# Second block of a fused two-block kernel: queries and keys projected and normed by token tile, taps queued behind fixed instructions, residual scaled on VectorE

## Chip, cores and metric

One core of a Trainium2 chip runs the whole program. The metric is the device time of one execution in microseconds; lower is better. The kernel before takes 1275.32 us (median of 3 runs, 1274.69 to 1275.57).

## What is computed

Two transformer blocks follow each other on 512 tokens of width 1024, in 32-bit floats. The change lies in the second block, up to its output projection:

```
h = rms_norm(x, norm1_g)
q, k, v, glu_a, glu_b = split(h @ w_in)           # 5 x 512 columns
q = rms_norm(q by head of 64, q_norm_g);  k the same with k_norm_g
attn = stick_breaking_attention(q, k, v)          # 8 heads, strictly causal
c = glu_a * sigmoid(glu_b)
c = causal_depthwise_conv(c, 31 taps);  c = silu(layer_norm(c))
x = x + concatenate([attn, c]) @ w_out
```

Here x is the first block's output, which ends in an rms norm of its own (final_norm_g); the kernel keeps it unnormed in `h` (tiles A) and multiplies by the token's factor later.

## The kernel before

Matrices are kept as a high and a low part (`copy_split`, `scale_split`), and a product of two of them is three matmuls (`mm3`, lines 123 to 125). Weights come by DMA into `raw` (two buffers), ScalarE casts them into `whi` (L195), VectorE subtracts to get `wlo` (L196); both have two buffers, so a cast waits until TensorE has read the last of an older weight tile. The token axis is the free axis of most tiles; queries and keys are first made with tokens on the partitions and then transposed.

In the second block `glu(i)` makes four 128-channel chunks of the gated product: 48 matmuls into a pair of PSUM banks, evacuation with the norm's factor (L693), sigmoid, product (L698) into `cc`. The convolution's 31 taps per chunk are one ScalarE instruction (L128) and 30 VectorE instructions (L832), each of which adds one tap to `cv[:, i, :]`; 120 in all, in an order that `conv` and `turns` give. `heads` makes queries (with `early[:2]` as weights, tiles F and G) and keys (tiles E and a fresh tile): `mov_stage` runs 96 matmuls for four token tiles of 128 into two pairs of banks, all four tiles for each half of the weights; then another `glu` (`between`) is issued; then for each pair of token tiles a square on ScalarE (L729), a sum by head on VectorE (L731), the power -0.5 on GpSimd in four instructions (L737 to L740, with the factors `rr` and `rr2` of the norm before), the product on VectorE (L741), eight transposes on TensorE (L745), and `scale_split` into the result (L139 on ScalarE, L140 on VectorE). Three PSUM pairs (`pair`) go round among all of these.

The attention stage behind it runs 12 steps (`seq`): `sticks` (scores, L774 and L779; abs, exponential and logarithm on ScalarE, L782 to L784; L785 and L132 on VectorE), `breaks` (L798, L801, exponential L803), `gather` (L813). Between them stand the remaining taps. `conv_norm` and `attended` (the output projection, L946 adds the residual) follow. The residual `h` is multiplied by `rb3`, the factor of the first block's last norm, in four GpSimd instructions (L871).

The program's order on each engine is made by the framework: it simulates the instructions as they are written and lets each engine take what is ready first; `tc.issue_after` puts an instruction behind another one in that order. Engines then run their queues in order, with waits on semaphores. The order is fixed when the program is built.

## Time and profile before

| | us |
|---|---|
| runs (median, lowest to highest of 3) | 1275.32 (1274.69 to 1275.57) |
| profiled execution | 1275.78 |
| its span, first to last instruction | 1274.1 |
| TensorE busy | 1257.1 |
| VectorE busy | 772.2 |
| ScalarE busy | 485.1 |
| GpSimd busy | 108.7 |

The second block's part up to the output projection lies between about 680 and 900 us of the span. In the timelines a row is: start, duration, engine, line, operation, output and inputs by tile, shapes, count of merged instructions, and in brackets the idle time ahead of it and who ended it. Matmuls overlap, so the distance between two starts, not a duration, is the rate. The granted clock (PEclk) is 1.00 at 2.4 GHz and 0.50 at 1.2 GHz.

### The profile page before, as it was taken

The page shows a single profiled execution, that of the slowest core. Times are in us where ns is not written, and L with a number is a line of the kernel's source. Part 1 is how long each engine was busy: PE and PEld are TensorE (multiplying, and loading weights), DVE is VectorE, ACT ScalarE, POOL GpSimd, SP SyncE. Part 2 cuts the span into 40 slices and gives each one's busy share as a digit, 9 for nine tenths or more (in the row PEclk, how much of TensorE's full clock was granted, in tenths as well). Part 3 has the DMA queues.
Part 4 walks back from the last instruction along what each step waited for, and adds up shares of the span by engine and source line. Part 5 has one row for each costly group of instructions (what it writes and reads, how often), then busy time and mean ns, then how long its engine had stood idle before and what let it go on. Part 6 is the DMA issues. An engine that isn't in the chain of part 4 may idle for free.

```text
span 1274.1 us, 13633 instructions
## 1 busy us (share of the span) xinstructions
PE 1257.1 (99%) x5712; PEld 1011.6 (79%) x5712; DVE 772.2 (61%) x813; ACT 485.1 (38%) x528; POOL 108.7 (9%) x125
## 2 busy tenths in 40 slices
PE   9999999999999999999999899999999999999998
PEld 6888888788888888888887678667888888888887
DVE  7845624744866664466366999976675555336522
ACT  6432524532544432243253225873443333213310
POOL 1100210012000000000054411000400000000000
PEclk9999999999999999999999989999999999999999
DMA  7233222312222222222343001101222222222212
GB/s 285 91 112 109 99 99 74 126 66 100 94 77 95 99 99 99 100 82 85 116 149 132 0 34 67 67 1 66 99 100 99 76 90 99 100 100 100 87 63 81
DMA packets 20445, 118.32 MB, mean 93 GB/s; under 512 B 2208, under 2 KB 4128, under 8 KB 7712
## 3 DMA queue, kind: packets, MB, share of 16 engines
q1 hardware_dynamic: 20096, 117.20, 26.1%
q8 instruction: 44, 0.72, 0.2%
q10 hardware_dynamic: 288, 0.26, 0.1%
q14 instruction: 17, 0.14, 0.0%
HBM read 115.35 MB, written 2.10 MB: 92 GB/s over the span
## 4 chain that ended last, share of the span: by engine, by line
PE 92%; DVE 4%; ACT 2%; issue 1%; POOL 1%; DMA 0%; SPq 0%; DVEq 0%; ACTq 0%
PE pp L124 28%; PE pp L125 28%; PE pp L123 28%; DVE H L832 2%; PE ps L123 1%; PE ps L124 1%; PE ps L125 1%; POOL col L739 0%; DVE H L698 0%; PE ps L317 0%; PE ps L813 0%; DVE t L785 0%; PE pp L774 0%; DMA A<-in_xT 0%; ACT t L783 0%
## 5 line engine op out<-in xcount | busy, mean ns | idle before, releaser
L195 ACT CAST whi<-raw 128x2048 fp32r<-128x2048 f32 (+3 forms) x109 | 197.8, 1815 | 452.4 <-PE pp L124 381.9
L196 DVE TENSOR_TENSOR wlo<-raw,whi 128x2048 fp32r<-128x2048 f32 (+3 forms) x109 | 236.8, 2173 | 73.2 <-ACT whi L195 72.6
L123 PE MATMUL pp<-B,whi 128*128 128x512 f32 x672 | 265.8, 397 | 1.0 <-ACT whi L195 1.0
L125 PE MATMUL pp<-B,wlo 128*128 128x512 f32 x672 | 266.3, 396 | 0.2
L124 PE MATMUL pp<-C,whi 128*128 128x512 f32 x672 | 266.0, 396 | 0.0
L124 PE MATMUL pp<-G,whi 128*128 128x512 f32 x448 | 177.8, 397 | 0.0
L125 PE MATMUL pp<-F,wlo 128*128 128x512 f32 x416 | 164.9, 396 | 0.0
L123 PE MATMUL pp<-F,whi 128*128 128x512 f32 x416 | 164.2, 396 | 0.0
L123 PEld LDWEIGHTS pp<-B,whi 128*128 128x128 f32 x672 | 126.3, 188 | 32.1 <-ACT whi L195 1.8
L125 PEld LDWEIGHTS pp<-B,wlo 128*128 128x128 f32 x672 | 126.2, 188 | 32.1 <-DVE wlo L196 1.5
L124 PEld LDWEIGHTS pp<-C,whi 128*128 128x128 f32 x672 | 126.3, 188 | 30.7 <-issue 0.5
L124 PEld LDWEIGHTS pp<-G,whi 128*128 128x128 f32 x448 | 84.2, 188 | 20.4 <-issue 0.2
L625 DVE TENSOR_TENSOR A<-pp,A 128x1024 f32<-128x1024 f32 x23 | 28.2, 1225 | 112.2 <-PE pp L125 112.2
L125 PEld LDWEIGHTS pp<-F,wlo 128*128 128x128 f32 x416 | 78.2, 188 | 19.0 <-issue 0.2
L646 DVE SCALAR_TENSOR_TENSOR H<-H,sm,H 128x512 f32<-128x512 f32 x132 | 92.8, 747 | 0.7
L123 PEld LDWEIGHTS pp<-F,whi 128*128 128x128 f32 x416 | 78.1, 188 | 19.0 <-issue 0.2
L832 DVE SCALAR_TENSOR_TENSOR H<-H,sm,H 128x512 f32<-128x512 f32 x120 | 88.3, 765 | 1.2
L651 DVE TENSOR_TENSOR H<-pp,rb 128x1024 f32<-128x1024 f32 x22 | 26.9, 1224 | 56.2 <-PE pp L125 49.8
L128 ACT ACTIVATE H<-H,sm 128x512 f32<-128x512 f32 x70 | 54.2, 808 | 9.8 <-DVE H L698 9.8
L997 DVE TENSOR_TENSOR H<-pp,rb 128x512 f32<-128x512 f32 x22 | 15.2, 692 | 67.7 <-PE pp L125 61.3
L124 PE MATMUL pp<-E,whi 128*128 128x512 f32 x112 | 44.3, 396 | 0.0
L123 PE MATMUL pp<-D,whi 128*128 128x512 f32 x112 | 44.2, 395 | 0.0
(293 smaller groups left out, 1808.8 us busy)
## 6 DMA issues: line engine op xcount, KB each, us to landing
raw<-in_wts SPq DMA_DIRECT2D x99, 1024.0 KB, 4.8
raw<-in_wts SPq DMA_DIRECT2D x8, 768.0 KB, 4.2
A<-in_xT SPq DMA_DIRECT2D x3, 512.0 KB, 6.8
out<-A SPq DMA_DIRECT2D x3, 512.0 KB, 2.8
D<-in_memT SPq DMA_DIRECT2D x1, 1024.0 KB, 11.6
raw<-in_wts SPq DMA_DIRECT2D x3, 256.0 KB, 7.1
A<-in_xT SPq DMA_DIRECT2D x2, 256.0 KB, 3.4
raw<-in_wts SPq DMA_DIRECT2D x2, 128.0 KB, 3.6
```

The lines of the kernel that those rows point to most:

```text
L123: pe.matmul(out, wh, xh, start=start, stop=False, **kw)
L124: pe.matmul(out, wh, xl, start=False, stop=False, **kw)
L125: pe.matmul(out, wl, xh, start=False, stop=stop, **kw)
L128: act.activation(out, in_, AF.Identity, scale=scale, bias=bias)
L195: act.copy(hi[:, cs], raw[:, cs])
L196: dve.tensor_tensor(lo[:, cs], raw[:, cs], hi[:, cs].bitcast(F32), ALU.subtract)
L625: dve.tensor_tensor(hu, pt, hu, ALU.add)
L646: dve.scalar_tensor_tensor(dst, hs[:, k : k + 512], w(k), dst, ALU.mult, ALU.add)
L651: dve.tensor_tensor(hs[:, :, 2:], pt, over2(rb), ALU.mult)
L832: tap = dve.scalar_tensor_tensor(cv[:, i, :], cc[:, i, k : k + 512], par("dw_w", 4 * k + i), cv[:, i, :], ALU.mult, ALU.add)
L997: dve.tensor_tensor(hs[:, 2:514], pt[:, 0, :], rb, ALU.mult)
```

## The change

`heads` now takes one token tile after the other (24 matmuls each, both halves of the weights) and issues square, sum, power and product for that tile at once, on 512 columns; GpSimd's four instructions become three with per-partition factors. `conv` takes its taps from one list, `TURNS`, which alternates between two chunks nearly throughout, and can be put behind a given instruction: 8 taps behind the first gated product, 6 behind the second, 5 behind each token tile's product of queries and keys and 5 behind the third and fourth gated product, the other 56 behind those. The residual's factor is applied on VectorE, written in `attended`. The diff, whole:

```diff
--- before.py
+++ after.py
@@ -695,7 +695,7 @@
         if i == 3:
             with tc.issue_after(sig.ins):
                 act.preload_act_table_set(tables)
-        dve.tensor_tensor(cc[:, i, 30:542], ab[:, 0, :], ab[:, 1, :], ALU.mult)
+        return dve.tensor_tensor(cc[:, i, 30:542], ab[:, 0, :], ab[:, 1, :], ALU.mult)
 
     rb2 = rb3 = None
 
@@ -716,33 +716,37 @@
 
     rr, rr2 = keep("rr"), keep("rr2")
 
-    def heads(name, gain, sc, between, early=()):
+    def heads(name, gain, sc, taps, between, early=()):
+
         gc = col(1)
         dve.tensor_scalar(gc, par(gain), sc, None, ALU.mult)
-        pts = mov_stage(ph, pl, NT, early)
+        ws = (list(early) + [weights() for _ in range(2 - len(early))])
         dst = [half(name + "0", 4, T), half(name + "1", 4, T)]
+        for t in range(NT):
+            if t % 2 == 0:
+                pt = pair()
+            ps = pt[:, t % 2, :]
+            st = slice(t * P, (t + 1) * P)
+            for k in range(KC):
+                wh, wl = (w[:, k % 4, :] for w in ws[k // 4])
+                mm3(ps, ph[:, k, st], pl[:, k, st], wh, wl, k == 0, k == KC - 1)
+            qn = norm2[:, t, :]
+            heads8 = qn.rearrange("p (b d) -> p b d", d=HD)
+            act.activation(qn, ps, AF.Square)
+            ms = tp.tile([P, 8], F32, tag="col16", name="col16", bufs=8)
+            dve.tensor_reduce(ms, heads8, AX.X, ALU.add)
+            pool.tensor_scalar(ms, ms, rr2[:, t : t + 1], EPS, ALU.mult, ALU.add)
+            pool.tensor_tensor(ms, ms, mhalf[:, :8], ALU.pow)
+            pool.tensor_scalar(ms, ms, rr[:, t : t + 1], None, ALU.mult)
+            conv(taps[t], dve.tensor_tensor(heads8, ps.rearrange("p (b d) -> p b d", d=HD),
+                                            ms.unsqueeze(2).to_broadcast([P, 8, HD]), ALU.mult))
         between()
         for i in range(2):
-            src = pts[i].rearrange("p a (b d) -> p (a b) d", d=HD)
-            qn = norm2[:, 2 * i : 2 * i + 2, :]
-            heads16 = qn.rearrange("p a (b d) -> p (a b) d", d=HD)
-            act.activation(qn, pts[i], AF.Square)
-            ms = col(16)
-            dve.tensor_reduce(ms, heads16, AX.X, ALU.add)
-            ms2 = ms.rearrange("p (a b) -> p a b", a=2)
-
-            def per_token(c):
-                return c[:, 2 * i : 2 * i + 2].unsqueeze(2).to_broadcast([P, 2, 8])
-
-            pool.tensor_tensor(ms2, ms2, per_token(rr2), ALU.mult)
-            pool.tensor_scalar(ms, ms, EPS, None, ALU.add)
-            pool.tensor_tensor(ms, ms, mhalf[:, :16], ALU.pow)
-            pool.tensor_tensor(ms2, ms2, per_token(rr), ALU.mult)
-            dve.tensor_tensor(heads16, src, ms.unsqueeze(2).to_broadcast([P, 16, HD]), ALU.mult)
             tr = pair().rearrange("p a (b c) -> p (a b) c", b=2)
             for t in range(2):
                 for hp in range(4):
-                    pe.transpose(tr[:, hp, t * P : (t + 1) * P], qn[:, t, hp * P : (hp + 1) * P], ident)
+                    pe.transpose(tr[:, hp, t * P : (t + 1) * P],
+                                 norm2[:, 2 * i + t, hp * P : (hp + 1) * P], ident)
             ts = slice(2 * i * P, (2 * i + 2) * P)
             scale_split(dst[0][:, :, ts], dst[1][:, :, ts], tr, gc)
         return dst
@@ -815,38 +819,34 @@
         copy_split(qT[0][:, hp, :], qT[1][:, hp, :], o)
 
 
+
+    TURNS = [0] * 8 + [0, 1] * 22 + [1, 2] * 8 + [2, 3] * 22 + [3] * 8
     done = [0] * 4
     tap = None
 
-    def conv(n, *chunks):
+    def conv(n, after=None):
 
         nonlocal tap
-        for _ in range(n):
-            for i in chunks:
-                k = done[i]
-                done[i] += 1
-                if k == 0:
-                    identity(cv[:, i, :], cc[:, i, 30:542], scale=par("dw_w", 4 * 30 + i),
-                             bias=par("dw_b", i))
-                with tc.issue_after(tap.ins) if tap else nullcontext():
-                    tap = dve.scalar_tensor_tensor(
-                        cv[:, i, :], cc[:, i, k : k + 512], par("dw_w", 4 * k + i), cv[:, i, :],
-                        ALU.mult, ALU.add)
+        tap = after or tap
+        for _ in range(min(n, len(TURNS))):
+            i = TURNS.pop(0)
+            k = done[i]
+            done[i] += 1
+            if k == 0:
+                identity(cv[:, i, :], cc[:, i, 30:542], scale=par("dw_w", 4 * 30 + i),
+                         bias=par("dw_b", i))
+            with tc.issue_after(tap.ins) if tap else nullcontext():
+                tap = dve.scalar_tensor_tensor(
+                    cv[:, i, :], cc[:, i, k : k + 512], par("dw_w", 4 * k + i), cv[:, i, :],
+                    ALU.mult, ALU.add)
 
     norm2 = half("D1", 4, T, F32)
-    glu(0)
+    conv(8, glu(0))
     split_early(2)
-    conv(10, 0)
-    turns = {1: ((20, 0, 1),), 2: ((10, 1, 2),), 3: ((20, 2), (30, 3))}
-
-    def gated(i):
-        glu(i)
-        for n, *chunks in turns[i]:
-            conv(n, *chunks)
-
-    gated(1)
-    qT = heads("G", "qg", HD ** -0.5, lambda: gated(2), early[:2])
-    kT = heads("F", "kg", 1.0, lambda: gated(3), early[2:])
+    conv(6, glu(1))
+    qT = heads("G", "qg", HD ** -0.5, (5, 5, 5, 5), lambda: conv(5, glu(2)), early[:2])
+    kT = heads("F", "kg", 1.0, (5, 5, 5, 5), lambda: conv(5, glu(3)), early[2:])
+    conv(120)
     v2 = half("E0", 4, T, F32)
     stk = {}
 
@@ -865,10 +865,6 @@
 
         at = (0, 1024 * (hp % 2), 768)[n]
         return part(place(6 if n == 1 else 4 + hp % 2), 2, WIDE[n], at)
-
-    for u in range(4):
-        hu = h[:, 2 * u : 2 * u + 2, :]
-        pool.tensor_tensor(hu, hu, over2(rb3), ALU.mult)
 
     cl = None
     ch = []
@@ -941,6 +937,8 @@
     def attended(u, after=None):
         pt = pair()
         half_out(u, qT[0], qT[1], [pt[:, j, :] for j in range(2)], after)
+        hu = h[:, 2 * u : 2 * u + 2, :]
+        dve.tensor_tensor(hu, hu, over2(rb3), ALU.mult)
         for j in range(2):
             c = 2 * u + j
             dve.scalar_tensor_tensor(h[:, c, :], h[:, c, :], par("g_fin", c), pt[:, j, :],
```

The built order, at the places that matter. First TensorE from the end of `glu(2)` (tiles B and C against whi, wlo) to the first key product, before. D holds the normed queries, F and G (or E) the weights of queries (or keys):

```order
L125 MATMUL pp<-B_4163,wlo 128x512
L745 MATMUL pp<-ident,D_4359 128x128 [waits DVE_49,Activation_49]
L745 MATMUL pp<-ident,D_4359 128x128 x7
L745 MATMUL pp<-ident,D_4359 128x128 [waits DVE_49,Activation_49]
L745 MATMUL pp<-ident,D_4359 128x128 x7
L123 MATMUL pp<-E_4458,B_4162 128x512 [waits DVE_49]
```

And with the change, at the same place, where the fourth query tile is still to come:

```order
L125 MATMUL pp<-B_4163,wlo 128x512
L748 MATMUL pp<-ident,D_4359 128x128 [waits DVE_49]
L748 MATMUL pp<-ident,D_4359 128x128 x3
L748 MATMUL pp<-ident,D_4359 128x128 [waits DVE_49,Activation_49]
L748 MATMUL pp<-ident,D_4359 128x128 x3
L123 MATMUL pp<-F_4113,B_4162 128x512 [waits DVE_49]
L124 MATMUL pp<-F_4114,B_4162 128x512
```

The transposes of tiles 0 and 1 stand between `glu(2)` and the 24 matmuls of tile 3; each of the three groups has a wait of its own for VectorE, and key products come behind the transposes of tile 2.

VectorE around the same place, before: sums (L731), taps (L832), products (L741), and only then the evacuation of `glu(2)` (L693) and the split of the next weights (L196).

```order
L731 TENSOR_REDUCE col_4757<-D_4359 128x16 [waits Activation_49]
L832 SCALAR_TENSOR_TENSOR H_2138<-H_2137,sm,H_2138 128x512 [waits DVE_49]
L731 TENSOR_REDUCE col_4776<-D_4359 128x16 [waits Activation_49]
L832 SCALAR_TENSOR_TENSOR H_2138<-H_2137,sm,H_2138 128x512 [waits DVE_49] x5
L741 TENSOR_TENSOR D_4359<-pp,col_4757 128x1024 [waits PE_49,Pool_49]
L832 SCALAR_TENSOR_TENSOR H_2138<-H_2137,sm,H_2138 128x512 [waits DVE_49] x3
L741 TENSOR_TENSOR D_4359<-pp,col_4776 128x1024 [waits PE_49,Pool_49]
L832 SCALAR_TENSOR_TENSOR H_2138<-H_2137,sm,H_2138 128x512 [waits DVE_49]
L693 TENSOR_TENSOR t_4731<-pp,rb 128x1024 [waits PE_49]
L832 SCALAR_TENSOR_TENSOR H_2138<-H_2137,sm,H_2138 128x512 [waits DVE_49]
L196 TENSOR_TENSOR wlo<-raw,whi 128x2048 [waits DMAHW2_49,Activation_49]
```

With the change (sums of tiles 1 and 2, then the third gated product and the split, then the products of tiles 1 and 2):

```order
L737 TENSOR_REDUCE col_4604<-D_4359 128x8 [waits Activation_49]
L737 TENSOR_REDUCE col_4641<-D_4359 128x8
L693 TENSOR_TENSOR t_4743<-pp,rb 128x1024 [waits PE_49]
L196 TENSOR_TENSOR wlo<-raw,whi 128x2048 [waits DMAHW2_49,Activation_49]
L698 TENSOR_TENSOR H_2137<-t_4743 128x512 [waits Activation_49]
L741 TENSOR_TENSOR D_4359<-pp,col_4604 128x512 [waits Pool_49]
L839 SCALAR_TENSOR_TENSOR H_2138<-H_2137,sm,H_2138 128x512 x2
L741 TENSOR_TENSOR D_4359<-pp,col_4641 128x512 [waits Pool_49]
L839 SCALAR_TENSOR_TENSOR H_2138<-H_2137,sm,H_2138 128x512 [waits DVE_49] x8
L737 TENSOR_REDUCE col_4677<-D_4359 128x8 [waits Activation_49]
L140 SCALAR_TENSOR_TENSOR G_4541<-pp,col_4538,G_4540 128x4x256 [waits PE_49,Activation_49]
```

The evacuation of `glu(2)` and the weight split moved ahead of the query products that the transposes wait for.

VectorE at the start of the stage, with the change (A holds the residual `h`; before, L698 stood right behind L693):

```order
L693 TENSOR_TENSOR t_4453<-pp,rb 128x1024 [waits Activation_49]
L693 TENSOR_TENSOR t_4527<-pp,rb 128x1024
L941 TENSOR_TENSOR A_76<-A_76,rb 128x1024 [waits Activation_49]
L941 TENSOR_TENSOR A_76<-A_76,rb 128x1024
L941 TENSOR_TENSOR A_77<-A_77,rb 128x1024 x2
L698 TENSOR_TENSOR H_2137<-t_4453 128x512 [waits Activation_49]
L698 TENSOR_TENSOR H_2137<-t_4527 128x512 [waits Activation_49]
L737 TENSOR_REDUCE col_4568<-D_4359 128x8 [waits Activation_49]
```

The four residual products stand here, though they are written in the output projection.

## Rows read from the trace of the kernel before

**Rows 1.** The page, part 1: busy time, share of the span and instructions of each engine.

```profile
PE 1257.1 (99%) x5712; PEld 1011.6 (79%) x5712; DVE 772.2 (61%) x813; ACT 485.1 (38%) x528; POOL 108.7 (9%) x125
...
PE 92%; DVE 4%; ACT 2%; issue 1%; POOL 1%; DMA 0%; SPq 0%; DVEq 0%; ACTq 0%
```

**Rows 2.** Busy time by stretch: the stretch, its length, then PE, PEld, DVE, ACT, POOL busy (instructions), granted clock, DMA share, GB/s.

```profile
728.00:732.00 4.00, 1.94 (x8) 1.57 (x8) 3.28 (x6) 0.34 (x1) 3.68 (x5) 0.62 0.00 0
...
736.00:740.00 4.00, 4.00 (x12) 3.16 (x11) 4.00 (x4) 0.94 (x2) 0.00 (x0) 0.60 0.24 61
740.00:744.00 4.00, 4.00 (x19) 3.25 (x18) 4.00 (x6) 0.82 (x1) 0.00 (x0) 1.00 0.48 201
```

**Rows 3.** Timeline of TensorE from the end of the third gated product to the first key products.

```profile
725.76 0.40 PE L125 MATMUL pp<-B,wlo 128*128 128x512 f32 x1
729.68 1.94 PE L745 MATMUL pp<-ident,D 128*128 128x128 f32 x8 [3.52 <-DVE D L741]
733.33 1.94 PE L745 MATMUL pp<-ident,D 128*128 128x128 f32 x8 [1.71 <-DVE D L741]
735.03 0.80 PE L123 MATMUL pp<-E,B 128*128 128x512 f32 x1
735.62 0.63 PE L124 MATMUL pp<-E,B 128*128 128x512 f32 x1
...
739.34 0.40 PE L124 MATMUL pp<-E,B 128*128 128x512 f32 x1
```

**Rows 4.** The same timeline earlier: two query matmuls that are 24 apart, and the first of the 48 of the third gated product (the last is the first row of rows 3).

```profile
698.47 0.39 PE L123 MATMUL pp<-G,B 128*128 128x512 f32 x1
...
703.91 0.39 PE L123 MATMUL pp<-F,B 128*128 128x512 f32 x1
...
714.80 0.39 PE L123 MATMUL pp<-B,whi 128*128 128x512 f32 x1
```

**Rows 5.** Timeline of VectorE at the start of the stage, and an ordinary L698 and tap later.

```profile
698.71 5.77 DVE L698 TENSOR_TENSOR H<-t 128x512 f32<-128x512 f32 x2 [0.91 <-ACT t L694]
704.40 2.89 DVE L832 SCALAR_TENSOR_TENSOR H<-H,sm,H 128x512 f32<-128x512 f32 x1
...
741.47 0.68 DVE L698 TENSOR_TENSOR H<-t 128x512 f32<-128x512 f32 x1
```

**Rows 6.** Timeline of GpSimd at the same time.

```profile
696.35 10.40 POOL L871 TENSOR_TENSOR A<-A,rb 128x1024 f32<-128x1024 f32 x4 [8.51 <-ACT rb L338]
```

**Rows 7.** The chain that ended last, in order of time (start, duration, what): two taps in a row on one chunk, and eleven on two chunks in turn.

```profile
707.33 0.76 DVE H L832
708.12 0.76 DVE H L832
...
714.42 7.38 DVE H L832 x11
```

**Rows 8.** VectorE's groups by line and shape, 690 to 790 us: count, busy us, mean ns, idle ahead and who ended it.

```profile
L196 DVE TENSOR_TENSOR wlo<-raw,whi 128x2048 fp32r<-128x2048 f32 x4 | 9.2, 2288 | 3.6 <-ACT whi L195 3.6
...
L741 DVE TENSOR_TENSOR D<-pp,col 128x1024 f32<-128x1024 f32 x4 | 4.9, 1224 | 1.4 <-POOL col L740 1.4
L731 DVE TENSOR_REDUCE col<-D 128x16 f32<-128x1024 f32 x4 | 4.9, 1215 | 2.3 <-ACT D L729 2.3
...
L140 DVE SCALAR_TENSOR_TENSOR G<-pp,col,G 128x1024 fp32r<-128x1024 f32 x2 | 2.6, 1278 | 0.0
```

**Rows 9.** GpSimd's groups, whole span.

```profile
L739 POOL TENSOR_TENSOR col<-col,mhalf 128x16 f32<-128x16 f32 x4 | 13.6, 3395 | 0.3
...
L325 POOL TENSOR_TENSOR col<-col,mhalf 128x4 f32<-128x4 f32 x6 | 6.1, 1015 | 111.3 <-DVE col L899 94.0 <-DVE col L320 13.3 <-DVE col L710 2.8
```

**Rows 10.** ScalarE's groups, 690 to 860 us.

```profile
L195 ACT CAST whi<-raw 128x2048 fp32r<-128x2048 f32 x6 | 11.4, 1908 | 26.7 <-PE pp L124 17.6 <-issue 8.2 <-PE ps L125 0.7
...
L729 ACT ACTIVATE D<-pp 128x1024 f32<-128x1024 f32 x4 | 4.1, 1025 | 23.7 <-PE pp L125 23.7
...
L139 ACT ACTIVATE G<-pp,col 128x1024 fp32r<-128x1024 f32 x2 | 2.2, 1113 | 6.3 <-PE pp L745 6.3
```

**Rows 11.** Timeline of VectorE at the end of queries and keys: the last ten taps of this stage and the first score instruction.

```profile
781.38 7.71 DVE L832 SCALAR_TENSOR_TENSOR H<-H,sm,H 128x512 f32<-128x512 f32 x10
790.12 0.96 DVE L785 SCALAR_TENSOR_TENSOR t<-pp,t 128x768 f32<-128x768 f32 x1 [1.03 <-ACT t L784]
```

**Rows 12.** Busy time by stretch in the attention stage, columns as in rows 2.

```profile
820.00:830.00 10.00, 8.18 (x54) 5.59 (x51) 9.93 (x14) 9.13 (x12) 0.00 (x0) 1.00 0.00 0
830.00:840.00 10.00, 8.66 (x64) 6.40 (x63) 9.86 (x13) 9.89 (x13) 0.00 (x0) 1.00 0.01 2
```

**Rows 13.** VectorE's groups by line and shape, 790 to 852 us.

```profile
L832 DVE SCALAR_TENSOR_TENSOR H<-H,sm,H 128x512 f32<-128x512 f32 x42 | 31.3, 747 | 0.5
...
L132 DVE TENSOR_TENSOR G<-ps,G 128x512 fp32r<-128x512 f32 x3 | 2.1, 687 | 0.0
```

**Rows 14.** Timeline of VectorE at the end of the attention stage.

```profile
844.46 3.11 DVE L832 SCALAR_TENSOR_TENSOR H<-H,sm,H 128x512 f32<-128x512 f32 x4
847.49 1.22 DVE L785 SCALAR_TENSOR_TENSOR t<-pp,t 128x1024 f32<-128x1024 f32 x1
848.62 0.74 DVE L832 SCALAR_TENSOR_TENSOR H<-H,sm,H 128x512 f32<-128x512 f32 x1
```

**Rows 15.** Timeline of TensorE there: the last pair of L801.

```profile
856.52 0.68 PE L801 MATMUL pp<-C,negtri 128*128 128x512 f32 x2
```

## The prediction

> **What bounds the kernel now.** The page first: TensorE is busy in 1257.1 of 1274.1 us and is 92% of the chain [rows 1]. A change can gain only where TensorE waits or runs slowly, so I looked for those places. The windows show one: between 728 and 740 us the granted clock is 0.62 and 0.60, and by 740 it is 1.00 again [rows 2]. TensorE's timeline says why. The third gated product (`glu(2)`) ends at 726.16; the first transposes of the queries start at 729.68 after 3.52 us idle, the second at 733.33 after 1.71, each released by VectorE's L741. The eight take 1.94 us, and the products behind them start 0.43 apart until 739.34 (735.62 to 739.34 holds nine steps, the last already faster), against 0.227 before [rows 3, 4]. That is TensorE's lower level, 1.2 GHz, after an idle stretch; it holds for some 5.7 us after work resumes.
>
> Second place: the attention stage. From 820 to 840 VectorE is busy 9.93 and 9.86 of 10 us while TensorE is busy 8.18 and 8.66 [rows 12]. There VectorE sets the pace: scores, splits and what is left of the 120 taps (L832) share it. At 790.12, where its first score instruction starts, 78 taps are done and 42 are left [rows 11, 13]. Its last score instruction (I call its end D) ends at 848.71 [rows 14]; from then on TensorE has output products to fill with.
>
> Third: VectorE's start of the stage. Two 128x512 products (L698) take 5.77 us and the first tap 2.89, where ordinary ones take 0.68 and 0.75, while GpSimd runs L871 from 696.35 to 706.75 [rows 5, 6]. This costs VectorE about 6.5 us.
>
> **The change, step by step.** I follow the built order of the change by hand from 698.47, up to where both orders agree, with this trace's durations.
>
> *Residual scaling.* GpSimd's four L871 go, and the 6.5 us with them. Four VectorE instructions come (L941), 128x1024 in 32 bits: L741 and L731 of that size take 1.22 [rows 8], so 4.9 us. Despite the title they stand right behind L693, not in the output projection. Gain on VectorE: 1.6 us, spent before the first gap. GpSimd was waited for by nobody there.
>
> *Norm by token tile.* Each of the four 1024-wide sums and products per side becomes two of 512. A 512-wide one takes 0.69 [rows 13], so a pair costs 1.38 for 1.22: eight pairs, +1.3 us, inside VectorE's holes below. GpSimd's power on 8 columns: not in the trace; 16 columns take 2.9 (mean 3.4 with one slow), 4 take 1.0 [rows 9]; between, I take 1.7; either end moves one wait by 0.7 to 1.2.
>
> *Nothing else.* ScalarE's squares become eight of about 0.6 us for four of 1.03 [rows 10], +0.7 us, while it is idle most of this stage; if it were not, the squares would lie in front of the casts and add as much. The weight loads on SP's queue keep their number and order; the casts behind them wait for TensorE's last reader, not for the load, as the third product's does in both orders.
>
> *First gap.* The order is now query tile 0, tile 2, 39 products of `glu(2)`, tile 1, the last nine of `glu(2)`. Tile 1 waits for tile 0's L741, done near 708, and starts at 713.05: no wait. A tile is 24 x 0.227 = 5.45 us, `glu` products come 0.233 apart [rows 3, 4]; TensorE ends `glu(2)` near 720.6. Tile 0's transposes wait for `glu(2)`'s evacuation; tile 1's wait for its L741, and that stands on VectorE behind L196. The split needs ScalarE's cast, which needs the last reader of its weight buffer, the end of `glu(2)`. So 1.91 (cast) + 2.29 (split) + 0.68 (L698) + 0.69 (L741) [rows 8, 10, 13] = 5.6: 726.3. Tile 3 waits further for tile 2's L741, behind two taps: 728.3. Three waits with 1.0 to 1.4 us of transposes between, in place of 5.2 idle before. Then tile 3 runs at the low level as above: 13 products 0.427 apart, 11 at 0.227, to 736.4.
>
> *Second gap, new.* The first key tile needs the buffer of the first transposes, and their ScalarE evacuation stands behind tile 3's square: 0.6 (half of L729) + 1.11 (L139) + 1.28 (L140) [rows 8, 10] = 3.0. Keys start at 739.6. Before they started at 735.03 at low rate, worth 737.1 at full rate, with no query transposes left to do.
>
> *Keys.* 23 products, 4 transposes, 25, 23 of `glu(3)`, 24: 22.3 us, so key tile 1 ends at 761.9. VectorE had only its fixed instructions and 15 taps for this time and stands idle from about 756 to 762.8. Then square, two sums, GpSimd 2.8: VectorE goes on at 766.7. From here its queue holds 24.3 us of work without a wait, to 791.0. So it comes to the attention stage 0.9 us later than before (790.1), **with 64 taps done in place of 78**. Its holes from 718 to 767 add to some 19 us by this count. TensorE reaches the same work 4.4 us late.
>
> *Attention.* D now has 56 taps before it where it had 41 (the 42nd came after it): 15 x 0.67 = +10.0; 0.67 is 7.38/11 of alternating chunks [rows 7]. The taps now alternate between two chunks; taps in a row on one chunk start 0.79 apart [rows 7, 14]. Before, 16 such steps lay in this stretch (runs of 2, 3 and 4, the last the row at 844.46): 16 x 0.12 = -1.9. At the end the new queue has fewer taps between scores, so VectorE waits there for ScalarE's three functions of the last head (1.0 each at 1024 columns, as the square [rows 10]): following the last six score instructions I get 3.5 us of holes. D = 848.7 + 0.9 + 10.0 - 1.9 + 3.5 = 861.2.
>
> The Trainium skill, "VectorE: DVE Perf Modes", section "The DRAIN you can't avoid", says that the pipeline flush after each instruction cannot be skipped and that a semaphore between chained instructions costs nothing extra. The rows differ: 0.79 with a wait on the tap just before, 0.67 without. By the page's rule the 1.9 would be no gain and the sum 13.0.
>
> *Tail.* From D to the end of TensorE's last L801 pair were 8.4 us (857.1) [rows 15]; now 9.0, but with 34 output products issued by then where there were 25: 9 x 0.233 = 2.1 fewer left. Net -1.4.
>
> **Sum:** 0.9 + 10.0 - 1.9 + 3.5 - 1.4 = +11.1 us. The profiled execution took 1275.78; 1286.9. The median shown, 1275.32, is 0.46 lower, so I say **1286.4**.
>
> **Rivals.**
> *The clock falls a second time (slower still).* For: the new 2.7 us without products at 737 comes soon after the first; 3.52 us idle brought the low level [rows 2, 3]. Against: ten us with only 8.18 busy kept 1.00 [rows 12]. Price: the slow stretch at 733 to 739 cost 1.07 for the transposes (1.94 for 0.87) and ten products x 0.2, so 3.1; it goes straight through keys to D: 1289.5. [...] Chance 0.12.
> *The backlog is hidden.* If ScalarE or TensorE sets the attention stage, the taps cost nothing and only TensorE's 4.4 us stay: 1279.7. For: ScalarE is busy 9.89 of 10 in 830 to 840. Against: VectorE is 9.93 in 820 to 830 where ScalarE has 9.13 [rows 12]. Chance 0.09.
> *Faster: the first gap stays shut.* It would if tile 1's product came before `glu(2)` ends, that is, were not held by the split; the point is L741 before 720.6. Then about 12.3 us of TensorE's lost time go (7.7 to 728.3 less 1.0 of transposes, 2.7 at 737, 2.6 of low rate and small ones), keys end near 750, D is at 849, and without the holes at the end the net is -4.7: 1270.6. Against: VectorE starts its queue in order, and the cast cannot start earlier. Chance 0.05.
> *The flush rule holds* (no gain from alternating): 1288.3. The rows speak against it. Chance 0.03.
>
> **How the numbers follow.** Forecast 0.71, the rivals 0.29 together. About 0.2%, 2.6 us, is what a measurement of this kernel tells from no change: 1272.8 to 1277.9. Below it lies the third rival and a little error of my count: 0.06. Inside it, a backlog half hidden with smaller gaps: 0.06. Slower 0.88. The range: the uncertain prices are the holes at the end (0 to 5), the low stretch (0 to 3 more) and GpSimd's power (0.7 to 1.2), which give 1282 to 1291; taking in the hidden backlog in part and the second fall with its error, 1279 to 1293.
>
> **What would show it.** Right: idle on TensorE between about 720 and 728 with the clock low behind it; a wait of some 2.7 us ahead of the first key product; VectorE idle some 6 us ahead of a key sum near 760; 64 taps done at the second key evacuation (L140) near 791, 78 not before 800; TensorE's busy share in the attention stage lower than before; L698 near 0.68 and no L871. Wrong: keys starting before 737, or over 75 taps done by 791, or VectorE idle several us in the middle of the attention stage.

## The result, and the profile after

The changed kernel takes 1291.87 us (median of 4 runs, 1291.38 to 1293.26); the kernel before, run beside it, 1275.44 us. The ratio is 1.013, 95% interval 1.0112 to 1.0147: 16.4 us slower, where +11.1 was forecast. The profiled execution took 1293.26 us, its span 1290.5 (1274.1 before).

The page, parts 1 and 4, answers to [rows 1]: TensorE does the same 5712 matmuls and is busy 7.9 us longer, so about half of the 16.4 us is slow running and the rest idle time.

```profile
PE 1265.0 (98%) x5712; PEld 1017.2 (79%) x5712; DVE 766.7 (59%) x825; ACT 486.4 (38%) x532; POOL 105.5 (8%) x129
...
PE 89%; DVE 7%; POOL 1%; issue 1%; ACT 1%; DMA 0%; SPq 0%; DVEq 0%; ACTq 0%
```

TensorE's timeline answers to [rows 3]: first from the end of `glu(2)` to the first key product, then at the first step of the attention stage.

```profile
720.97 0.40 PE L125 MATMUL pp<-B,wlo 128*128 128x512 f32 x1
722.68 0.66 PE L748 MATMUL pp<-ident,D 128*128 128x128 f32 x4 [1.32 <-DVE t L693]
727.01 1.09 PE L748 MATMUL pp<-ident,D 128*128 128x128 f32 x4 [3.67 <-ACT H L128]
729.14 0.80 PE L123 MATMUL pp<-F,B 128*128 128x512 f32 x1 [1.04 <-DVE D L741]
...
740.66 0.50 PE L123 MATMUL pp<-E,B 128*128 128x512 f32 x1 [2.57 <-DVE G L140]
...
807.53 0.62 PE L802 MATMUL pp<-D,negone 128*128 128x128 f32 x1
810.57 0.58 PE L802 MATMUL pp<-D,negone 128*128 128x256 f32 x1 [2.42 <-DVE t L789]
812.10 0.48 PE L802 MATMUL pp<-D,negone 128*128 128x128 f32 x1 [0.94 <-DVE D L132]
```

In the brackets are the waits that were forecast: 1.32 and 3.67 us ahead of the transposes of tiles 0 and 1, 1.04 ahead of tile 3, and 2.57 ahead of the keys. The second bracket names ScalarE's L128; VectorE's L741 of tile 1, which the forecast named, ended at the same time (726.86, below). The last two rows were not forecast: TensorE waits 3.4 us for the first two score instructions.

The windows (columns as in [rows 2]) show the granted clock behind each of these waits.

```profile
728.00:732.00 4.00, 2.96 (x8) 2.31 (x8) 3.79 (x7) 0.00 (x0) 0.36 (x1) 0.50 0.39 162
...
740.00:744.00 4.00, 3.33 (x10) 2.70 (x11) 3.04 (x5) 0.00 (x0) 1.44 (x2) 0.74 0.00 0
...
808.00:812.00 4.00, 0.74 (x3) 0.29 (x1) 4.00 (x6) 3.49 (x5) 0.00 (x0) 0.77 0.52 150
812.00:816.00 4.00, 3.90 (x17) 3.57 (x19) 4.00 (x5) 1.15 (x2) 0.00 (x0) 0.50 0.52 150
...
820.00:824.00 4.00, 4.00 (x16) 3.86 (x16) 4.00 (x6) 2.72 (x4) 0.00 (x0) 0.52 0.02 6
```

There are three stretches at the lower level: one from about 727, a short one in 740 to 744 (products 0.43 apart from 741.9 to 744.9), and 810 to 823. The kernel before had the first alone.

VectorE's timeline answers to [rows 5], [rows 11] and [rows 14].

```profile
698.34 4.62 DVE L941 TENSOR_TENSOR A<-A,rb 128x1024 f32<-128x1024 f32 x4
702.88 1.29 DVE L698 TENSOR_TENSOR H<-t 128x512 f32<-128x512 f32 x2
...
704.68 3.10 DVE L839 SCALAR_TENSOR_TENSOR H<-H,sm,H 128x512 f32<-128x512 f32 x4
...
723.15 2.29 DVE L196 TENSOR_TENSOR wlo<-raw,whi 128x2048 fp32r<-128x2048 f32 x1 [0.52 <-ACT whi L195]
...
726.17 0.69 DVE L741 TENSOR_TENSOR D<-pp,col 128x512 f32<-128x512 f32 x1
...
728.39 0.69 DVE L741 TENSOR_TENSOR D<-pp,col 128x512 f32<-128x512 f32 x1 [0.21 <-POOL col L740]
...
738.32 0.69 DVE L737 TENSOR_REDUCE col<-D 128x8 f32<-128x512 f32 x1 [3.94 <-ACT D L735]
...
765.66 1.28 DVE L737 TENSOR_REDUCE col<-D 128x8 f32<-128x512 f32 x2 [7.77 <-ACT D L735]
...
787.35 0.69 DVE L741 TENSOR_TENSOR D<-pp,col 128x512 f32<-128x512 f32 x1 [2.26 <-POOL col L740]
...
794.58 1.28 DVE L140 SCALAR_TENSOR_TENSOR F<-pp,col,F 128x1024 fp32r<-128x1024 f32 x1
795.78 8.16 DVE L839 SCALAR_TENSOR_TENSOR H<-H,sm,H 128x512 f32<-128x512 f32 x12
803.85 0.95 DVE L789 SCALAR_TENSOR_TENSOR t<-pp,t 128x768 f32<-128x768 f32 x1
...
864.16 1.22 DVE L789 SCALAR_TENSOR_TENSOR t<-pp,t 128x1024 f32<-128x1024 f32 x1 [2.39 <-ACT t L788]
```

L698 and the first taps are short again behind the four L941 (4.62 us). The split L196 stands ahead of the products of tiles 1 and 2, as in the built order. Further down are the holes that the fixed queue leaves: 3.94 and 7.77 us ahead of sums, 2.26 ahead of the last key product. The second key evacuation ends at 795.86 (I call this K), 12 taps stand between it and the first score at 803.85, and the last score ends at 865.38 (D).

GpSimd's timeline, to [rows 9]: L738 and L740 ordinarily take 0.3 us.

```profile
720.72 0.27 POOL L738 TENSOR_SCALAR col<-col,rr 128x8 f32<-128x8 f32 x1 [12.60 <-DVE col L737]
...
723.20 2.94 POOL L740 TENSOR_SCALAR col<-col,rr 128x8 f32<-128x8 f32 x1
...
781.66 3.49 POOL L738 TENSOR_SCALAR col<-col,rr 128x8 f32<-128x8 f32 x1 [10.21 <-DVE col L737]
```

The long ones, 2.94 and 3.49 us, end with VectorE's two-input instructions beside them: the split L196 from 723.15 with the L698 behind it to 726.05, and two taps from 781.49 with the split behind them to 785.09.

To follow where time goes I split each trace into 2 us windows and add up TensorE's loss: idle is the window's length less PE busy, slow is busy time x (1 - granted clock). The table holds all kernels; the experiments are told below.

```
kernel            median  taps ahead of    K     first    D     loss 720-796  loss 796-880
                    us    first score           score           idle + slow   idle + slow
before           1275.44      78         781.5  790.1  848.7     5.2 + 3.8     4.3 + 0.0
after            1291.87      76         795.9  803.9  865.4    10.0 + 5.2     7.2 + 6.1
e1 more taps     1300.17      92         795.6  804.1  879.8     9.9 + 4.2    12.3 + 7.4
e2 tiles only    1323.91     118         811.6  819.4  902.8    18.6 + 7.0    16.1 + 7.0
e3 taps only     1277.98      54         771.1  779.7  852.0     0.0 + 0.0     8.7 + 4.9
e4 residual only 1277.44      73         773.5  782.8  851.5     0.1 + 0.0     8.6 + 3.1
e5 more, pinned  1289.32      92         795.9  804.4  864.2     9.9 + 5.3     5.9 + 6.1
e6 14 left out   1292.14      76         794.8  802.8  865.5     9.9 + 4.9     8.2 + 5.1
e7 glu mid       1299.55      85         797.3  806.5  874.4    12.7 + 5.7     7.0 + 10.2
e8 alt, residual 1272.04      76         773.3  782.5  843.2     1.2 + 0.0     5.4 + 1.6
e9 glu(3) last   1301.88      66         789.3  797.8  878.1    15.6 + 7.4     9.5 + 3.3
e10 split late   1292.90      76         792.0  799.9  867.1     7.5 + 4.3     9.5 + 8.0
e11 combined     1298.59      75         786.2  795.0  870.0    14.0 + 6.1     7.1 + 4.6
e12 held         1289.54      78         795.1  801.1  862.5     9.9 + 5.3     8.2 + 1.6
```

From 690 to 910 the loss is 13.3 us before and 28.5 after: 15.2 of the 16.4 us by which the span grew. It grew by 6.2 in the heads and by 9.0 in the attention stage.

### The profile page after: what moved, and what is told of

Read it like the earlier page. It is cut to its first block, busy times and chain, and to the rows that moved or that the text cites. A ratio compares the mean times of both kernels' runs of the same rounds, so it can differ in the third digit from the quotient of the medians.

```text
span 1290.5 us, 13655 instructions
## 1 busy us (share of the span) xinstructions
PE 1265.0 (98%) x5712; PEld 1017.2 (79%) x5712; DVE 766.7 (59%) x825; ACT 486.4 (38%) x532; POOL 105.5 (8%) x129
## 4 chain that ended last, share of the span: by engine, by line
PE 89%; DVE 7%; POOL 1%; issue 1%; ACT 1%; DMA 0%; SPq 0%; DVEq 0%; ACTq 0%
PE pp L123 28%; PE pp L124 28%; PE pp L125 28%; DVE H L839 4%; PE ps L123 1%; PE ps L125 1%; PE ps L124 1%; POOL col L739 1%; PE pp L805 1%; PE pp L802 1%; PE ps L817 0%; PE ps L317 0%; DVE wlo L196 0%; DVE t L789 0%; POOL col L738 0%
## 5 line engine op out<-in xcount | busy, mean ns | idle before, releaser
L196 DVE TENSOR_TENSOR wlo<-raw,whi 128x2048 fp32r<-128x2048 f32 (+3 forms) x109 | 237.6, 2181 | 72.4 <-ACT whi L195 72.0
L646 DVE SCALAR_TENSOR_TENSOR H<-H,sm,H 128x512 f32<-128x512 f32 x132 | 92.7, 747 | 0.7
L839 DVE SCALAR_TENSOR_TENSOR H<-H,sm,H 128x512 f32<-128x512 f32 x120 | 83.4, 745 | 0.4
L128 ACT ACTIVATE H<-H,sm 128x512 f32<-128x512 f32 x70 | 54.2, 808 | 9.4 <-DVE H L698 9.4
L995 DVE TENSOR_TENSOR H<-pp,rb 128x512 f32<-128x512 f32 x22 | 15.2, 692 | 67.2 <-PE pp L125 61.9
```

Of the source, the lines that this page charges most:

```text
L128: act.activation(out, in_, AF.Identity, scale=scale, bias=bias)
L196: dve.tensor_tensor(lo[:, cs], raw[:, cs], hi[:, cs].bitcast(F32), ALU.subtract)
L646: dve.scalar_tensor_tensor(dst, hs[:, k : k + 512], w(k), dst, ALU.mult, ALU.add)
L839: tap = dve.scalar_tensor_tensor(cv[:, i, :], cc[:, i, k : k + 512], par("dw_w", 4 * k + i), cv[:, i, :], ALU.mult, ALU.add)
L995: dve.tensor_tensor(hs[:, 2:514], pt[:, 0, :], rb, ALU.mult)
```

## Experiments

The theory to begin with was the prediction's, called the backlog below: the quotas of taps leave VectorE holes, and the taps that do not stand there are left over for a stage that VectorE sets. Its rival was that TensorE's gaps and slow stretches set the end by themselves. The diffs are cut to the lines that matter and are against the change unless they say otherwise.

**e1, more taps in the holes.**

```diff
-(5, 5, 5, 5), lambda: conv(5, glu(2))
+(5, 5, 10, 5), lambda: conv(5, glu(2))
-(5, 5, 5, 5), lambda: conv(5, glu(3))
+(14, 5, 5, 0), lambda: conv(10, glu(3))
```

> The changed kernel with larger quotas of taps where its VectorE stands idle: 10 behind query tile 2 (was 5), 14 behind key tile 0 (was 5), 10 behind the fourth gated product (5), none behind key tile 3 (5). 79 taps stand ahead of the second key evacuation where 64 did; nothing else moves. Theory (the taps left over for the attention stage set the end): VectorE's wait of 7.8 us ahead of the key sum and that of 3.9 us ahead of the third query sum shrink by 14 x 0.67 = 9.4 us together, D and the end come 9.4 us earlier, 1282.5 us (1281 to 1285). Rival (TensorE's gaps and its three stretches at the lower clock set the end): these stay, and the time stays within 1.5 us of 1291.9.

Measured: 1300.17 us, ratio to before 1.0191 (1.0175 to 1.0206). Neither expectation came. The hole ahead of the key sum shrank from 7.77 to 1.68, but with the convolution done early the built order put its norm, and the silu in it, among the scores. ScalarE's timeline:

```profile
858.99 1.28 ACT L905 ACT_TABLE_LOAD   x1
860.28 0.81 ACT L905 ACTIVATE H<-H,sm 128x512 f32<-128x512 f32 x1
861.12 1.28 ACT L788 ACT_TABLE_LOAD   x1
```

Nine table loads lie between 770 and 905 where the change has two (seven more; the expectation of e5 says eight): 7 x 1.28 = 9 us of ScalarE's time. With this second difference the run tells nothing on the theories, so e5 repeats it without.

**e2, heads by token tile alone** (against before: `heads` as in the change; taps, their freedom and L871 as before).

```diff
-    qT = heads("G", "qg", HD ** -0.5, (5, 5, 5, 5), lambda: conv(5, glu(2)), early[:2])
+    qT = heads("G", "qg", HD ** -0.5, lambda: gated(2), early[:2])
```

> The kernel before with the heads by token tile alone: the taps in the order and with the freedom of before, the residual on GpSimd. TensorE's order is nearly that of the change, so its gaps at about 721 to 729 and 737 to 740 come back with the low clock behind them. VectorE's holes are filled with taps (83 ahead of the first key evacuation, 108 ahead of the second; with the change 49 and 64). Theory (backlog of taps): 1276 to 1283 us, most of the loss gone though the gaps stay. Rival (gaps and clock): as the change, 1288 to 1293.

Measured: 1323.91 us, 1.0377 (1.0361 to 1.0392): 48 us slower, far beyond both. VectorE's timeline, then TensorE's:

```profile
715.67 11.34 DVE L837 SCALAR_TENSOR_TENSOR H<-H,sm,H 128x512 f32<-128x512 f32 x17
726.93 1.27 DVE L737 TENSOR_REDUCE col<-D 128x8 f32<-128x512 f32 x2
728.12 1.21 DVE L693 TENSOR_TENSOR t<-pp,rb 128x1024 f32<-128x1024 f32 x1
```

```profile
729.38 1.12 PE L748 MATMUL pp<-ident,D 128*128 128x128 f32 x4 [6.64 <-DVE t L693]
```

Seventeen free taps stand ahead of the query sums, and `glu(2)`'s evacuation behind them: TensorE waits 6.64 us for it. The run also has 13 table loads more than before (16.6 us of ScalarE's time), so the 48 us are not the price of the tiles alone. With heads by tile, then, the kernel with free taps ends later than the one with quotas, in the orders that were built.

**e3, taps alone** (against before: `TURNS` and quotas of 10 behind each pair's product).

```diff
-            dve.tensor_tensor(heads16, src, ms..., ALU.mult)
+            conv(taps[i], dve.tensor_tensor(heads16, src, ms..., ALU.mult))
```

> The kernel before with the list of taps and the quotas of the change alone (10 behind each pair's product), the heads by pairs of tiles and the residual on GpSimd as before. No tap stands ahead of the query products any more, so TensorE's first gap (5.2 us idle and some 3 us of low clock) should shrink; 41 taps stand ahead of the second key evacuation where 68 did, 54 ahead of the first score instruction where 78 did. Theory (backlog): 24 taps more in the attention stage, 24 x 0.67 = 16 us, less 2 for alternating chunks: 1288 to 1291 us. Rival (gaps and clock): 1268 to 1273, as the gap shrinks.

Measured: 1277.98 us, 1.0025 (1.0013 to 1.0037). With 24 taps fewer ahead of the first score the kernel loses 2 us, not 13. Its window, columns as above:

```profile
720.00:740.00 20.00, 20.00 (x96) 16.32 (x95) 14.99 (x17) 5.27 (x5) 5.86 (x6) 1.00 0.14 53
```

TensorE has no gap at all in 720 to 740 and the first score comes 10.4 us early; the attention stage then lasts 72 us from first score to D, where the kernel before had 59. What was won was given back there, in a stage with 64 taps left in place of 41, where VectorE is busy for 71.1 of 72.2 us (row below, with the account of the prediction).

**e4, residual alone** (against before).

```diff
-    for u in range(4):
-        hu = h[:, 2 * u : 2 * u + 2, :]
-        pool.tensor_tensor(hu, hu, over2(rb3), ALU.mult)
...
+        hu = h[:, 2 * u : 2 * u + 2, :]
+        dve.tensor_tensor(hu, hu, over2(rb3), ALU.mult)
```

> The kernel before with the residual's factor on VectorE alone. VectorE loses 4.9 us to the four products and wins 6.5 us of the stretched first products: 1.6 us earlier. But the built order now has 73 taps ahead of the first score instruction where 78 stood. Theory (backlog): up to 1.6 us gained at the start, up to 5 x 0.67 = 3.4 us lost if VectorE idles for them: 1274 to 1278. Rival (GpSimd's products cost nothing, since VectorE's start is not on the path): 1275.4 within 1 us.

Measured: 1277.44 us, 1.0013 (1.0004 to 1.0022).

```profile
720.00:740.00 20.00, 19.88 (x95) 16.18 (x94) 19.27 (x24) 5.26 (x5) 5.58 (x6) 1.00 0.16 53
```

TensorE's gap closes here too, and the gain is given back in the attention stage (a loss of 11.7 us in the table, where the kernel before has 4.3). So neither the quotas nor the residual alone makes the loss, which leaves the heads by token tile. The quotas and the residual together, without the heads by token tile, were not run.

**e5, e1 with the norm of the convolution kept behind the scores.**

```diff
+            with tc.issue_after(score.ins):
                 dve.scalar_tensor_tensor(ci, mu, -1.0 / 512.0, ci, ALU.mult, ALU.add)
...
+            with tc.issue_after(weighted.ins):
                 act.activation(ci, ci, AF.Silu, ...)
```

> As e1 (14 more taps in VectorE's holes), with the first step of the convolution's norm issued behind the last score instruction and its silu behind the last exponential, as stands in the change; in e1 they had moved among the scores and brought eight more table loads of 1.28 us on ScalarE. Theory (VectorE's work plus its holes set D, and the end comes 424 to 425 us behind D): holes shrink by up to 9.4 us, D 856, end 1281 to 1283. Rival (the stage is bound from its first score on, by ScalarE and TensorE; the first score started at 804.1 in e1 and 803.9 with the change, and the 1024-wide score that follows stood 3 us apart): D 861 to 865, end 1286 to 1290.

Measured: 1289.32 us, 1.0104 (1.0089 to 1.0119), D 864.2: the rival's numbers. Sixteen taps more ahead of the first score are worth 2.6 us, not 10. The two added lines are called pins below.

**e6, the last 14 taps left out.**

```diff
-    TURNS = ... + [2, 3] * 22 + [3] * 8
+    TURNS = ... + [2, 3] * 19
```

> The change with the last 14 taps left out (part of the convolution is not computed), the norm of the convolution pinned as in e5. VectorE's queue is the same up to about 846 us, so its holes, TensorE's gaps and the three stretches at the low clock up to there stay. Theory (backlog): 14 x 0.67 = 9.4 us less VectorE work before D, of which the waits for ScalarE take back a part: 1281 to 1286. Rival (gaps and clock alone): 1290 to 1292.

Measured: 1292.14 us, 1.0129 (1.0114 to 1.0144): nothing gained. For the change the backlog theory falls. VectorE's timeline at the end:

```profile
849.60 1.22 DVE L792 SCALAR_TENSOR_TENSOR t<-pp,t 128x1024 f32<-128x1024 f32 x1 [3.18 <-ACT t L790]
...
864.31 1.23 DVE L792 SCALAR_TENSOR_TENSOR t<-pp,t 128x1024 f32<-128x1024 f32 x1 [3.19 <-ACT t L790]
```

Where taps stood VectorE now waits for ScalarE, and the last two 1024-wide scores start 14.7 us apart; with taps between them, in the change, 13.2. So from score to score there is a chain of other work, by the program's order score, split, L802 and L805 (the change's lines), exponential and the next scores, that is no shorter without taps.

**e7, the gated product after tile 2.**

```diff
+            if t == 2:
+                between()
...
-        between()
         for i in range(2):
```

> The change with the gated product that stands between the heads' products and their transposes written behind the second token tile, so that the products of tiles 2 and 3 stand behind it; quotas as they are. The product L741 of tile 1 and the split no longer stand between TensorE and its transposes: the waits at 721 to 729 and 738 to 741 should go, and with them VectorE's holes of 3.9 and 7.8 us. Theory: D back to 847 to 851, end 1271 to 1276. Rival (the quotas and the norm by tile cost by themselves): 1283 or more.

Measured: 1299.55 us, 1.018 (1.0163 to 1.0198): the theory was wrong. TensorE's waits moved and did not go (3.65 and 2.16 us ahead of the transposes and tile 3), and the heads lose 18.4 us where the change loses 15.2.

**e8, the two other parts together** (against before: e4, the alternating list without quotas, the first pin of e5).

```diff
-    turns = {1: ((20, 0, 1),), 2: ((10, 1, 2),), 3: ((20, 2), (30, 3))}
+    TURNS = [0] * 8 + [0, 1] * 22 + [1, 2] * 8 + [2, 3] * 22 + [3] * 8
```

> The kernel before with two parts of the change, free of quotas: the residual on VectorE and the taps in the alternating order, with the norm of the convolution pinned behind the last score (in e4 it had moved ahead of D and put 2.5 us of other work there). Theory: VectorE 1.6 us earlier at the start and 1.9 us by the alternating taps, D some 3 us earlier, end 1271 to 1274. Rival (D is set by ScalarE or TensorE by then): 1275 to 1277.

Measured: 1272.04 us, 0.9973 (0.996 to 0.9985): 3.6 us faster than before, as expected, and the fastest kernel here.

```profile
720.00:740.00 20.00, 19.22 (x92) 15.69 (x91) 19.27 (x24) 5.26 (x5) 4.61 (x6) 1.00 0.15 53
```

The gap at 728 is 0.8 us, and the attention stage, in which e3 and e4 lost 13.6 and 11.7, loses 7.0. Of the change's parts these two, with the pin, are the ones to keep. How the 3.6 us divide between the alternating list and the pin was not tried.

A second theory came from these: K sets the first score, and from there the stage takes its 59 to 62 us. The kernel before, the change, e5, e6 and e8 gave 58.6 to 62.8; e4 and e7, with 68.7 and 67.9, did not fit it even then.

**e9, `glu(3)` behind the keys.**

```diff
-    kT = heads(..., lambda: conv(5, glu(3)), early[2:])
+    kT = heads(..., lambda: None, early[2:], lambda: conv(5, glu(3)))
```

> The change with the fourth gated product written behind the transposes of the keys, in place of ahead of them; quotas as they are. On TensorE its 48 products (11.2 us) then stand behind the last key tile. New theory (the end of the second key evacuation, K, sets the first score, and from there to D the stage takes 59 to 62 us however many of up to 44 taps are left, and half a us more for each tap beyond): K 785 to 788 in place of 795.9, first score 794 to 797, 54 taps left, D 858 to 862, end 1283 to 1287. Backlog theory: VectorE's holes do not shrink and more taps are left, 1291 to 1295. Rival (TensorE's gaps and clock alone): nothing in them changes ahead of 760, 1290 to 1292.

Measured: 1301.88 us, 1.0223 (1.0187 to 1.0258). K came 6.6 us earlier and D 12.8 later, so the second theory was wrong. `glu(3)` had covered the key products' chain of square, sum, power and product; without it TensorE waits 4.72 and 1.62 us for L741 among the keys, and two table loads more stand between 770 and 905.

**e10, one split later.** In `prep` the low part that is made while `glu(2)` runs is issued behind query tile 2's product.

```diff
+            with tc.issue_after(behind[0].ins) if behind and not late else nullcontext():
                 dve.tensor_tensor(lo[:, cs], raw[:, cs], hi[:, cs].bitcast(F32), ALU.subtract)
```

> The change with one instruction moved: the split L196 of 2.3 us that stands on VectorE between the third gated product's evacuation and the products L741 of query tiles 1 and 2 goes behind these. GpSimd's L740, held for 2.9 us while that split ran, should take 0.3. TensorE's second wait (3.7 us) falls by the split's 2.3 and the L698 behind it stays. All theories agree here on the sign; it sizes the place: K and the end 2.5 to 4 us earlier, 1288 to 1289.5, and if the short gap leaves the clock up, another 2 to 3.

Measured: 1292.90 us, 1.0137 (1.0121 to 1.0153): K and the first score are 3.9 us earlier, as expected, and the end is not. GpSimd's step was freed as expected (L745 here is L740 of the change); then VectorE's timeline near the end:

```profile
722.65 0.31 POOL L745 TENSOR_SCALAR col<-col,rr 128x8 f32<-128x8 f32 x1
```

```profile
856.22 2.48 DVE L890 SCALAR_TENSOR_TENSOR H<-ps,H 128x512 f32<-128x512 f32 x4 [1.43 <-PE ps L886]
...
865.85 1.23 DVE L797 SCALAR_TENSOR_TENSOR t<-pp,t 128x1024 f32<-128x1024 f32 x1 [2.06 <-ACT t L796]
```

The built order had put the convolution's norm (L890 here, 2.48 us, and three L894) ahead of the last scores. Whether that alone took the 3.9 us back was not tried.

**e11, e9 and e10 together**, with quotas (5, 6, 8, 6) and (8, 7, 5, 5) and the pins of e5.

> e9 and e10 together, quotas of 5, 6, 8, 6 and 8, 7, 5, 5, and the norm of the convolution pinned as in e5. New theory: K 782 to 786, some 10 taps more ahead of the first score than in e9, D 850 to 856, end 1275 to 1281: most of the loss gone, with the heads by token tile kept. Backlog theory: holes shrink by the taps alone, 1284 to 1288.

Measured: 1298.59 us, 1.0179 (1.0162 to 1.0195): both theories were wrong. The first score is 8.9 us earlier than with the change, D 4.7 later. VectorE's timeline between the second score and the third:

```profile
801.77 8.70 DVE L852 SCALAR_TENSOR_TENSOR H<-H,sm,H 128x512 f32<-128x512 f32 x13
810.39 2.28 DVE L199 TENSOR_TENSOR wlo<-raw,whi 128x2048 fp32r<-128x2048 f32 x1
...
813.92 2.28 DVE L199 TENSOR_TENSOR wlo<-raw,whi 128x2048 fp32r<-128x2048 f32 x1
...
818.07 1.23 DVE L802 SCALAR_TENSOR_TENSOR t<-pp,t 128x1024 f32<-128x1024 f32 x1 [0.55 <-ACT t L800]
```

The builder filled this stretch with 20 taps and two splits; the third score starts at 818.07, with the change it started at 816.36. Score by score the lead was lost before the third.

**e12, taps held behind the second score** (against e5). A third theory: TensorE runs dry at the first scores. In the built order before, 48 matmuls that make the values (`project`) stand between the first scores' products and the first L798; with the change 24, since the others had filled the wait for the keys.

```diff
-    conv(120)
...
     sticks(*seq[1])
+    conv(120, score)
```

> e5 with one thing moved: the taps that are left (41) are held behind the second score instruction, so that 8 taps in place of 22 stand among the products, key evacuation and first two scores; the rest of VectorE's queue has the same instructions. Third theory (TensorE ran dry at the first scores: it waited 3.4 us for them with no value products left to fill, and its clock was at the lower level from 810 to 823 behind that): first score at 801 to 802 in place of 804.4, the wait ahead of the first L805 under 1.5 us, the granted clock 1.00 from 808 to 824, and the end 5 to 9 us earlier than e5: 1280 to 1284. Rival (the stage holds as much VectorE work as before, only later in it): D 862 to 865, 1287 to 1290.

Measured: 1289.54 us, 1.0108 (1.009 to 1.0125), the same as e5 to within the noise.

```profile
808.00:812.00 4.00, 2.20 (x17) 1.95 (x19) 4.00 (x5) 3.75 (x5) 0.00 (x0) 1.00 0.51 213
812.00:816.00 4.00, 4.00 (x38) 3.47 (x38) 4.00 (x6) 1.50 (x2) 0.00 (x0) 1.00 0.74 262
816.00:820.00 4.00, 2.71 (x15) 1.53 (x14) 4.00 (x6) 2.84 (x5) 0.00 (x0) 1.00 0.03 6
```

The local part was right: the first score starts at 801.1, the wait is 1.35 us, and the clock is 1.00 throughout 808 to 824, where e5 ran slowly. In the table its slow running falls from 6.1 to 1.6 us. The end was the rival's: VectorE is busy 4.00 of 4 here, TensorE waits for it instead (its idle time grows from 5.9 to 8.2), and D moved by 1.7 us.

## Why the prediction came out as it did

The kernel is slower, as forecast, and in the heads the times came out nearly as forecast. Step by step:

*Residual.* The forecast was 1.6 us gained on VectorE, 6.5 us of stretching less 4.9 of new work. Measured are 4.62 us for L941, 1.29 for two L698 and 3.10 for four taps, in place of 5.77 for the two L698 and 2.89 for the first tap alone. Counting one tap at 0.75 that is 6.7 in place of 8.7, so 2.0 gained: right. That TensorE's gap could close by this part alone, and that the attention stage would give the gain back, I had not seen (e4).

*First gap.* The stage starts 0.6 us later in this execution. The releases were forecast at 726.3 and 728.3 and came at 727.01 and 729.14, behind the split as said; the second had 0.21 us more in it, since tile 2's L741 waited for GpSimd. Thirteen products behind it ran slowly, as said.

*Second gap.* The wait was 2.57 us where 2.7 was said, and the keys start at 740.66 for 739.6.

*The clock's second fall* was a rival with a chance of 0.12. It came, and cost some eight products x 0.2 = 1.6 us where its price was 3.1. With it and the later keys VectorE goes on at 769.3 (forecast 766.7). A third fall, 810 to 823, was in no case. The 1291.87 measured lies nearer to this rival's 1289.5 than to the forecast's 1286.4. Not every wait brought a fall: behind the 1.35 us in e12 the granted clock stayed at 1.00.

*VectorE's queue.* 64 taps were done at the second key evacuation, as said; it starts at 794.6 (forecast 791.0). Of the 3.6 us 0.6 are from the start and 2.0 from the keys and their slow products. The rest is a hole of 2.26 that was left out, behind the GpSimd instruction of 3.49 us, less 1.2 us of work that was counted too many. The Trainium skill's "SBUF — State Buffer", section "SBUF: two separate sides", says that a VectorE instruction with two SBUF inputs, if it starts first, holds the port pair that it shares with GpSimd for its whole length, and that a GpSimd instruction which reads SBUF is blocked by it. The rows of 2.94 and 3.49 us for 0.3 agree, and e10, where the first of them fell to 0.31 with the split moved. I had read that lock in one direction alone, from [rows 5] and [rows 6].

*Attention.* As a length of VectorE's queue the forecast came out: from the start of the second key evacuation to D it was 70.2 us (791.0 to 861.2), and it took 70.8, the first row below (VectorE's busy time is the third of the engines). As a price per tap, "15 x 0.67 = +10.0", this step failed. The other rows go from the first score to D: before, the change, e3, e5, e6, e12.

```profile
794.58:865.38 70.80, 63.63 (x369) 46.30 (x368) 66.99 (x87) 54.78 (x64) 0.00 (x0) 0.90 0.09 30
...
790.12:848.70 58.58, 54.28 (x351) 38.86 (x350) 57.02 (x70) 50.51 (x60) 0.00 (x0) 1.00 0.11 37
803.85:865.38 61.53, 54.36 (x317) 38.98 (x316) 57.76 (x74) 48.73 (x58) 0.00 (x0) 0.89 0.10 35
779.72:851.96 72.24, 64.16 (x369) 46.41 (x368) 71.13 (x94) 50.82 (x60) 0.00 (x0) 0.93 0.09 30
804.44:864.22 59.78, 54.24 (x321) 38.88 (x320) 48.08 (x58) 47.14 (x57) 0.00 (x0) 0.89 0.10 36
802.78:865.54 62.76, 54.66 (x327) 38.54 (x326) 48.80 (x60) 49.67 (x59) 0.00 (x0) 0.92 0.10 34
801.06:862.53 61.47, 53.31 (x326) 37.12 (x325) 56.46 (x71) 50.42 (x59) 0.00 (x0) 0.97 0.10 35
```

In e3, where VectorE is full, the price fits: 23 taps more than before make the stage 13.6 us longer, and 23 x 0.67 less the 1.9 for alternating chunks gives 13.5. In the change it does not: e5 and e6 have 9.7 and 9.0 us less VectorE work in the stage, and D moved by -1.2 and +0.2 us. Something else in the stage is about as long as VectorE's queue. D came out at +16.7 for +12.5: the first score stands 13.7 us later, and from it to D the stage takes 61.5 us for 58.6. That the sum came near is in part luck, since "64 taps done at 791" says in taps what K says in time: the keys are late.

*The other rivals.* The hidden backlog (0.09) had its premise right for the last taps (e6) and its time, 1279.7, wrong, since it has no loss in the attention stage. The flush rule (0.03) did not come: alternating taps start 0.67 us apart here too (twelve in 8.16 us).

*Tail.* The forecast was -1.4 us, measured are -0.3 (from D to the end 425.1 us for 425.4).

**What is shown:** the loss comes with the heads by token tile. Without them the kernels with the quotas (e3), with the residual (e4) and with residual and alternating taps (e8) take 1272 to 1278 us, and every kernel with them takes 1289 or more; quotas and residual together without them were not run. In the change the tap backlog is not what sets the end (e5, e6), and TensorE's loss accounts for 15.2 of the 16.4 us. **What stays open:** the cause of the 9.0 us in the attention stage, that is, why D holds at 862 to 867 in e5, e6, e10 and e12. Backlog, keys and clock were each relieved there, but one at a time: e5 and e6 took work off VectorE with the clock low (6.1 and 5.1 us of slow running), e12 kept the clock up with VectorE busy for 56.5 of 61.5 us. A kernel with both was not run. VectorE's queue, the chain from score to score and TensorE's waits lie within a few us of each other there, and each edit made the builder order the rest anew.

## What to carry to other kernels

A stage in which an engine is nearly always busy need not be set by that engine alone: leave some of its instructions out before pricing the rest, since a chain about as long can lie beside it, as here in the change but not in e3. Cutting a unit of work finer only helps if each piece's dependent steps still have other work on TensorE to hide under; here TensorE idled 5.2 us in the heads with the coarse order and 10.0 with the fine one. When a builder sets the order, look at what moved far from the edit (here a silu among exponentials, 7 and 13 table loads) before reading a time.

## What was not expected of the hardware

A GpSimd instruction on 128x8 elements, 0.27 to 0.32 us by itself, took 2.94 and 3.49 us while VectorE ran a 128x2048 subtraction and its neighbour, and 0.31 in e10 with the subtraction moved. Nine us of TensorE's time won back ahead of 770 (e3, e4) were worth nothing at the end of the next stage. A kernel with its clock kept at 1.00 in a stretch where another had 0.50 (e12 and e5) lost 4.5 us less to slow running, idled 2.3 us more behind a busier VectorE, and ended at the same time.
